# Folding the key projection into the query's, and running the first merge group's projections as three products of halves

## The chip, the core and the metric

The kernel runs on one core of one Trainium2 chip. TensorE (PE) multiplies matrices into PSUM, VectorE (DVE) and ScalarE (ACT) read PSUM and SBUF, GpSimd (POOL) works on SBUF, SyncE (SP) issues most of the transfers. Each engine takes its instructions in the order in which the program lists them, and waits on semaphores for the others. The metric is the device time of the whole kernel in microseconds (us), as a median of runs.

## What is computed

One encoder layer over 1024 tokens of 1024 channels. Only what the change touches is shown; `h` is the normalised input, the chunkwise scan uses `q` and `k` through their inner products and through a state that is a sum of `k v`.

```python
q = jnp.einsum("bshd,hde->bhse", xc, w_q)                    # 4 heads, d = e = 256
k = jnp.einsum("bshd,hde->bhse", xc, w_k) / math.sqrt(d)
v = jnp.einsum("bshd,hde->bhse", xv, w_v)
s = jnp.einsum("bhtd,bhsd->bhts", qc, kc) * w_intra          # in mlstm_scan, chunks of 128
num = w_inter * einsum(qc, C) + einsum(s, vc)                # C_new = decay * C + k w_state v
...
merged = g_m * (y_m @ w_branch_mlstm) + g_l * (y_l @ w_branch_lru)
x = x + merged @ w_out
q = rms_norm(x) @ peer_w_q                                   # 1024 -> 2048, then key scores, top-k
```

## The kernel before

The program is written through a tile framework that orders the instructions of each engine with a model of its own before the run; what stands on each engine is fixed when the kernel is built. All channels lie on the 128 partitions, tokens along the free axis.

**Halves.** Where products must be more exact than one pass of reduced fp32 allows, an operand is split in two: `split` (lines 73 to 79) makes the high half on ACT (or DVE) and the low half, source minus high, on DVE or POOL. `mm3` (lines 81 to 86) then issues three matmuls: high x high (L84), high weight x low (L85), low weight x high (L86). A plain fp32 matmul is one instruction of the program and leaves two records in the trace.

**Weights.** `ws_plan`, `ws_load`, `ws_split` and `ws_get` (lines 89 to 132) stream all weight blocks through a ring of three raw tiles (`wr`) and a ring of high and low tiles (`wh`, `wl`; three deep in the mixers, two deep, `WB2`, from the merge on). A call for block i issues the load of block i + 2 and the split of block i + 1. An entry of the plan that names no engine is handed out raw.

**Mixers.** After the LRU come four mLSTM heads. For each head `ml_x` projects and convolves two 128-channel blocks into `xc`, splits them, and `ml_qkv` makes q, k and v: q and k from one 1024-wide weight tile (`mwq` and `mwk` side by side) with 24 matmuls of 512 columns each, evicted by ACT at line 582, then v with 48 matmuls of 256 columns. `ml_core` runs the chunks; its recurrence leaves PE free at places, and output and merge-gate projections (`ml_o`, `mg`) are put there.

**Merge.** The tokens are then taken in three groups, `GROUPS = [(0, 2), (2, 3), (5, 3)]`, in blocks of 128: group 0 has 256 tokens, the others 384. `merge` runs four projections on a group, with 8, 8, 8 and 16 column blocks of weights (bm, bl, wo, wq), each block eight fp32 matmuls in `mm8` (line 851). Gate tiles, input tiles and keys are loaded beside them by SP. Group 0 runs alone; beside groups 1 and 2 the top-k and one-hot work of dense blocks (`side`) is put on DVE and PE. The dense stage with the gathers, from about 1685 us on, isn't touched.

Of the kernel before, what the change touches and what calls it, by code (L numbers as in the profile page):

```python
# [21 lines left out]
NB = 8  # L22
# [12 lines left out]
class K:  # L35
# [506 lines left out]
    def ml_x(self, h, done=None):  # L542

        nc = self.nc
        st = {}
        st["xm"], st["xc"] = [], []
        for e in range(2):
            blk = 2 * h + e
            x = self.pad_proj(blk, done if e == 0 else None)
            hi, lo = self.u(F32R), self.u(F32R)  # L550
            self.split(x[:, 2:2 + S], hi[:, :S], lo[:, :S])
            st["xm"].append((hi, lo))
            xc = self.u()
            self.conv(xc, x, V_MCW, V_MCB, blk)

            def act(xc=xc):
                nc.scalar.activation(xc[:, :S], xc[:, :S], AF.Silu)
                hi, lo = self.u(F32R), self.u(F32R)
                self.split(xc[:, :S], hi[:, :S], lo[:, :S])
                st["xc"].append((hi, lo))  # L560

            if e == 0:
                act()
            else:
                self.later = act
        return st

    def ml_qkv(self, h, st):
        nc = self.nc
        wh, wl = self.ws_get(("qk", h))  # L570
        for i, nm in enumerate(("q", "k")):
            st[nm] = []
            for e in range(2):
                t = self.u()
                for hf in range(2):
                    c = slice(hf * 512, hf * 512 + 512)
                    p = self.psg()
                    for cb in range(2):
                        o = i * 512 + cb * 256 + e * 128
                        self.mm3(p, (wh[:, o:o + 128], wl[:, o:o + 128]),  # L580
                                 (st["xc"][cb][0][:, c], st["xc"][cb][1][:, c]), cb == 0, cb == 1)
                    nc.scalar.activation(t[:, c], p, AF.Copy, scale=1.0 if i == 0 else 1.0 / 16.0)
                st[nm].append(t)
# [164 lines left out]
    def mixer_plan(self):  # L748
# [29 lines left out]
        for s_ in seq:  # L778
            if s_[0] == "x":
                inw(2 * s_[1])  # L780
                inw(2 * s_[1] + 1)
            elif s_[0] == "o":
                inw(8 + 2 * s_[1])
                inw(9 + 2 * s_[1])
            elif s_[0] == "mg":
                inw(32 + s_[1])
            elif s_[0] == "qkv":
                h = s_[1]
                plan.append((("qk", h), [(self.A["mwq"][h], 512), (self.A["mwk"][h], 512)], 1024, WENG))
# [42 lines left out]
    def merge_items(self, g):  # L832
        A = self.A
        it = []
        for nm, n in (("bm", 8), ("bl", 8), ("wo", 8)) + (("wq", 16),) * len(QSPLIT[g]):
            it += [((nm, g, i), [(A[nm][i], 1024)], 1024, None) for i in range(n)]
        return it

    def load_y(self, src, t0, T):
        r = []  # L840
        for i in range(4):
            t = self.u()
            self.dma = self.nc.sync.dma_start(t[:, :2 * T].rearrange("p (c t) -> p c t", t=T),
                                              src[2 * i:2 * i + 2, :, t0:t0 + T].rearrange("c p t -> p c t"))
            r.append(t)
        return lambda cb: r[cb // 2][:, (cb % 2) * T:(cb % 2) * T + T]

    def mm8(self, p, w, m):

        for cb in range(NB):  # L850
            self.nc.tensor.matmul(p, w[:, cb * 128:cb * 128 + 128], m(cb), start=cb == 0, stop=cb == NB - 1)  # L851

    def merge(self, g, b0, nb):

        nc = self.nc
        T, t0 = nb * 128, b0 * 128
        pair = lambda lst, d: lst[d // 2][:, (d % 2) * T:(d % 2) * T + T]
        y = self.load_y(self.ym_d, t0, T)
        mt = []
        for d in range(NB):  # L860
            if d % 2 == 0:
# [8 lines left out]
        y = self.load_y(self.yl_d, t0, T)  # L870
        for d in range(NB):
            gt = self.u()
            nc.sync.dma_start(gt[:, :T], self.mg_d[8 + d, :, t0:t0 + T])
            w = self.ws_get(("bl", g, d))
            p = self.ps()[:, :T]
            self.mm8(p, w, y)
            nc.vector.tensor_tensor(gt[:, :T], p, gt[:, :T], op=OP.mult)
            nc.vector.tensor_tensor(pair(mt, d), pair(mt, d), gt[:, :T], op=OP.add)
            yield 24 * T * 4.2e-4
        x1, hg = [], []  # L880
        for d in range(NB):
            if d % 2 == 0:
                x1.append(self.u())
                hg.append(self.u())
# [4 lines left out]
            self.mm8(p, w, lambda cb: pair(mt, cb))  # L889
            x = pair(x1, d)  # L890
            nc.vector.tensor_tensor(x, p, xt[:, :T], op=OP.add)
            nc.scalar.activation(pair(hg, d), x, AF.Copy, scale=self.vec(V_G2, d))
            yield 24 * T * 4.2e-4
        rs = self.rs2[:, b0:b0 + nb]
        g2r = []
# [51 lines left out]
        for q0, qn in QSPLIT[g]:  # L947
# [3 lines left out]
            for c in range(16):  # L951
# [7 lines left out]
                self.mm8(p, w, lambda d: pair(hg, d)[:, tq:tq + Tq])  # L959
# [592 lines left out]
def host(**i):  # L1552
# [10 lines left out]
    d["mwq"], d["mwk"], d["mwv"] = hw(a["mlstm_w_q"]), hw(a["mlstm_w_k"]), hw(a["mlstm_w_v"])  # L1563
# [30 lines left out]
```

## Time and profile before

| what | us |
|---|---|
| median of 3 runs (lowest to highest) | 3574.14 (3561.7 to 3575.13) |
| the profiled execution, its own time | 3566.02 |
| its span, first to last instruction | 3563.9 |
| PE busy | 3343.9 (94%) |
| DVE busy | 2929.6 (82%) |
| POOL busy | 1713.4 (48%) |
| ACT busy | 1392.0 (39%) |

The profile is of one execution, and its busy times are averages over stages: the mixers end at about 918 us, group 0 runs from 923 to about 1076 us, groups 1 and 2 to about 1685 us. What a change is worth is read in its own stage. PE's records are pipelined, so the pace of a run of matmuls is read from start to start, or from a row that merges many.

### The profile page before, as it was taken

The page shows a single profiled execution, that of the slowest core. Times are in us where ns is not written, and L with a number is a line of the kernel's source. Part 1 is how long each engine was busy: PE and PEld are TensorE (multiplying, and loading weights), DVE is VectorE, ACT ScalarE, POOL GpSimd, SP SyncE. Part 2 cuts the span into 40 slices and gives each one's busy share as a digit, 9 for nine tenths or more (in the row PEclk, how much of TensorE's full clock was granted, in tenths as well). Part 3 has the DMA queues.
Part 4 walks back from the last instruction along what each step waited for, and adds up shares of the span by engine and source line. Part 5 has one row for each costly group of instructions (what it writes and reads, how often), then busy time and mean ns, then how long its engine had stood idle before and what let it go on. Part 6 is the DMA issues. An engine that isn't in the chain of part 4 may idle for free. (4 is left out here: it accounts for less than half of the span.)

```text
span 3563.9 us, 48538 instructions
## 1 busy us (share of the span) xinstructions
PE 3343.9 (94%) x17633; PEld 2827.0 (79%) x17633; DVE 2929.6 (82%) x5279; ACT 1392.0 (39%) x2565; POOL 1713.4 (48%) x1336
## 2 busy tenths in 40 slices
PE   7999999899899899878899999999999999999998
PEld 5787788778685565556788888998888999999987
DVE  8777574674327866998899999989999999999998
ACT  4565655655120240233333333343333334333333
POOL 7445354444102322342455555655555665666663
PEclk9999999999999999989899999999999999999999
DMA  2122211111466575558888879997887999999996
GB/s 107 60 71 68 72 51 51 63 48 44 154 217 208 159 251 199 174 170 258 312 318 301 283 275 342 360 338 276 314 284 279 341 357 351 344 347 334 352 348 239
DMA packets 319665, 812.56 MB, mean 228 GB/s; under 512 B 25600, under 2 KB 137408, under 8 KB 319424
## 3 DMA queue, kind: packets, MB, share of 16 engines
q0 software_dynamic: 115200, 419.48, 32.4%
q1 hardware_dynamic: 115184, 333.21, 26.7%
q10 hardware_dynamic: 89040, 56.76, 5.3%
q8 instruction: 138, 2.26, 0.3%
q14 instruction: 103, 0.84, 0.1%
HBM read 726.35 MB, written 83.00 MB: 227 GB/s over the span
## 5 line engine op out<-in xcount | busy, mean ns | idle before, releaser
L1334 POOL DMA_INDIRECT k<-in_pv,k x384 | 514.0, 1338 | 378.6 <-DVE k L1365 182.3
L1334 POOL DMA_INDIRECT k<-in_pu,k x384 | 506.6, 1319 | 332.7 <-DVE k L1357 148.0
L84 PE MATMUL ps<-h2h,wh 128*128 128x320 f32 x2048 | 637.2, 312 | 10.2 <-DVE u L1268 9.9
L85 PE MATMUL ps<-h2l,wh 128*128 128x320 f32 x2048 | 635.2, 310 | 0.0
L86 PE MATMUL ps<-h2h,wl 128*128 128x320 f32 x2048 | 628.9, 310 | 5.8 <-DVE wl L71 5.8
L851 PE MATMUL ps<-u,wr 128*128 128x384 f32 (+1 forms) x1920 | 581.1, 460 | 5.5 <-DMA u<-d 3.4
L1357 DVE SCALAR_TENSOR_TENSOR k<-k,rs,k 128x1024 f32<-128x1024 f32 x384 | 493.5, 1289 | 28.4 <-DMA k<-in_pu,k 28.4
L851 PEld LDWEIGHTS ps<-u,wr 128*128 128x128 f32 x1920 | 366.4, 194 | 181.7 <-issue 11.6
L85 PE MATMUL ps<-vl,wdh 128*128 128x512 f32 x1280 | 501.9, 393 | 2.5 <-DVE vl L71 2.5
L84 PE MATMUL ps<-vh,wdh 128*128 128x512 f32 x1280 | 469.0, 395 | 35.1 <-DVE u L1268 17.4
L1365 DVE SCALAR_TENSOR_TENSOR k<-k,k,k 128x1024 f32<-128x1024 f32 x384 | 494.6, 1288 | 0.4
L86 PE MATMUL ps<-vh,wdl 128*128 128x512 f32 x1280 | 494.3, 391 | 0.0
L84 PEld LDWEIGHTS ps<-h2h,wh 128*128 128x128 f32 x2048 | 388.1, 190 | 23.3 <-DVE u L1268 17.0
L86 PEld LDWEIGHTS ps<-h2h,wl 128*128 128x128 f32 x2048 | 385.6, 189 | 8.0 <-DVE wl L71 6.3
L85 PEld LDWEIGHTS ps<-h2l,wh 128*128 128x128 f32 x2048 | 387.8, 189 | 4.5
L1195 ACT ACTIVATE gel<-ps 128x320 f32<-128x320 f32 x256 | 111.1, 435 | 564.2 <-PE ps L86 549.4
L84 PEld LDWEIGHTS ps<-vh,wdh 128*128 128x128 f32 x1280 | 239.3, 189 | 88.2 <-DVE u L1268 22.5
L84 PE MATMUL ps<-h,wh 128*128 128x512 f32 x736 | 292.3, 399 | 14.0 <-ACT u L430 6.7
L86 PE MATMUL ps<-h,wl 128*128 128x512 f32 x736 | 290.8, 396 | 3.5 <-POOL wl L71 3.5
L85 PE MATMUL ps<-h,wh 128*128 128x512 f32 x736 | 291.0, 396 | 2.8 <-DVE h L253 2.8
L1238 ACT ACTIVATE gc<-gt 128x160 f32<-128x160 f32 x512 | 226.3, 510 | 155.9 <-DVE gel L1239 94.4
L86 PEld LDWEIGHTS ps<-vh,wdl 128*128 128x128 f32 x1280 | 241.4, 189 | 50.4
(327 smaller groups left out, 6079.1 us busy)
## 6 DMA issues: line engine op xcount, KB each, us to landing
wr<-in_u SPq DMA_DIRECT2D x128, 512.0 KB
wr<-in_v SPq DMA_DIRECT2D x128, 512.0 KB
d<-stg ACTq DMA_DIRECT2D x40, 1024.0 KB
gt<-d SPq DMA_DIRECT2D x64, 640.0 KB
wr<-in_win SPq DMA_DIRECT2D x49, 512.0 KB
wr<-in_wq SPq DMA_DIRECT2D x48, 512.0 KB
d<-u POOLq DMA_DIRECT2D x32, 512.0 KB
wr<-in_bm SPq DMA_DIRECT2D x24, 512.0 KB
```

Source lines behind the costliest of these rows:

```text
L84: mm(out, wh, mh, start=first, stop=False)
L85: mm(out, wh, ml, start=False, stop=False)
L86: self.lastmm = mm(out, wl, mh, start=False, stop=last)
L851: self.nc.tensor.matmul(p, w[:, cb * 128:cb * 128 + 128], m(cb), start=cb == 0, stop=cb == NB - 1)
L1195: nc.scalar.activation(gel[:, c], p, AF.Gelu)
L1238: nc.scalar.activation(gc[:, i * n:i * n + n], self.gt[j // 8, i][:, :, j % 8], AF.Copy)
L1334: nc.gpsimd.indirect_dma_start(out=t[:, :D], out_offset=None, in_=self.A["pu" if which == "u" else "pv"], in_offset=bass.IndirectOffsetOnA ...
L1357: nc.vector.scalar_tensor_tensor(r[:, :D], r[:, :D], self.rs2[:, b:b + 1], h2[:, :D], op0=OP.mult, op1=OP.mult, accum_out=dots[c][:, k % K ...
L1365: nc.vector.scalar_tensor_tensor(acc[:, :D], r[:, :D], ws[c][:, k % KB:k % KB + 1], acc[:, :D], op0=OP.mult, op1=OP.add)
```

## The change

Two edits. **In the mixers** the weights of q and k are stored transposed, `ml_qkv` multiplies them into one 256 x 256 matrix per head (four fp32 matmuls of 256 columns), ACT and DVE split it from PSUM with the factor 1/16, and q is projected through that matrix; `xc` itself then stands where k stood. The 24 matmuls of k, four of the eight evictions and the split of the 1024-wide weight tile (ACT and POOL) go. **In merge group 0** the weights are split (ACT high, DVE low), and so are the two branch inputs, the merged tiles and the scaled residual, and each fp32 matmul becomes three matmuls of halves. Groups 1 and 2 stay in fp32.

```diff
     def ml_qkv(self, h, st):
-        wh, wl = self.ws_get(("qk", h))
-        for i, nm in enumerate(("q", "k")):
...
-                        o = i * 512 + cb * 256 + e * 128
-                        self.mm3(p, (wh[:, o:o + 128], wl[:, o:o + 128]),
-                                 (st["xc"][cb][0][:, c], st["xc"][cb][1][:, c]), cb == 0, cb == 1)
-                    nc.scalar.activation(t[:, c], p, AF.Copy, scale=1.0 if i == 0 else 1.0 / 16.0)
+        raw = self.ws_get(("qk", h))
+        p = self.psg()
+        for cb in range(2):
+            for eb in range(2):
+                nc.tensor.matmul(p[:, cb * 256:cb * 256 + 256], raw[:, eb * 256 + cb * 128:eb * 256 + cb * 128 + 128],
+                                 raw[:, 512 + eb * 256:512 + eb * 256 + 256], start=eb == 0, stop=eb == 1)
+        t = self.u(F32R)
+        wh, wl = t[:, 0:512], t[:, 512:1024]
+        nc.scalar.activation(wh, p, AF.Copy, scale=1.0 / 16.0)
+        nc.vector.scalar_tensor_tensor(wl, p, 1.0 / 16.0, wh.bitcast(F32), op0=OP.mult, op1=OP.subtract)
...
-                plan.append((("qk", h), [(self.A["mwq"][h], 512), (self.A["mwk"][h], 512)], 1024, WENG))
+                plan.append((("qk", h), [(self.A["mwq"][h], 512), (self.A["mwk"][h], 512)], 1024, None))
...
-            it += [((nm, g, i), [(A[nm][i], 1024)], 1024, None) for i in range(n)]
+            it += [((nm, g, i), [(A[nm][i], 1024)], 1024, "v" if g == 0 else None) for i in range(n)]
...
     def load_y(self, src, t0, T, halves):
+            if halves:
+                hi, lo = self.u(F32R), self.u(F32R)
+                self.split(t[:, :2 * T], hi[:, :2 * T], lo[:, :2 * T])
+                t = (hi, lo)
...
     def mm8(self, p, w, m):
         for cb in range(NB):
-            self.nc.tensor.matmul(p, w[:, cb * 128:cb * 128 + 128], m(cb), start=cb == 0, stop=cb == NB - 1)
+            c = slice(cb * 128, cb * 128 + 128)
+            if isinstance(w, tuple):
+                self.mm3(p, (w[0][:, c], w[1][:, c]), m(cb), cb == 0, cb == NB - 1)
+            else:
+                self.nc.tensor.matmul(p, w[:, c], m(cb), start=cb == 0, stop=cb == NB - 1)
...
+            if halves:
+                if d % 2 == 0:
+                    mhl.append((self.u(F32R), self.u(F32R)))
+                self.split(pair(mt, d), *both(mhl, d))
...
+            if halves:
+                h, l = both(hhl, d)
+                nc.scalar.activation(h, x, AF.Copy, scale=self.vec(V_G2, d))
+                nc.vector.scalar_tensor_tensor(l, x, self.vec(V_G2, d), h.bitcast(F32), op0=OP.mult, op1=OP.subtract)
```

How the instructions stand on the engines, in three places.

PE before, second head: the last filler matmuls (`ps<-h`) and the start of q (`pg<-u` is q or k from the halves of `xc`).

```order
L84 MATMUL ps_4447<-h_444,wh_4228 128x512
L85 MATMUL ps_4447<-h_445,wh_4228 128x512
L84 MATMUL ps_4561<-h_444,wh_4228 128x512
L85 MATMUL ps_4561<-h_445,wh_4228 128x512
L84 MATMUL pg_4022<-u_3799,wh_3877 128x512
L85 MATMUL pg_4022<-u_3800,wh_3877 128x512
L86 MATMUL pg_4022<-u_3799,wl_3878 128x512
```

PE in the changed kernel, second head: the product of the two weight matrices (L576) between filler matmuls.

```order
L84 MATMUL ps_4501<-h_444,wh_4168 128x512
L576 MATMUL pg_3987<-wr_3776 128x256 x4
L85 MATMUL ps_4501<-h_445,wh_4168 128x512
L86 MATMUL ps_4501<-h_444,wl_4169 128x512
L84 MATMUL ps_4501<-h_450,wh_4168 128x512
```

Twenty-three filler matmuls stand between the product and the first q matmul, which reads the folded matrix (`u_3992`):

```order
L85 MATMUL ps_4501<-h_488,wh_4168 128x512
L86 MATMUL ps_4501<-h_487,wl_4169 128x512
L84 MATMUL pg_3996<-u_3769,u_3992 128x512
L85 MATMUL pg_3996<-u_3770,u_3992 128x512
L84 MATMUL pg_4004<-u_3769,u_3992 128x512
```

PE before, group 0, from the third column block of the first projection on: one block after the other (`ps` a block's sum, `wr` its raw weights, `u` the loaded branch input).

```order
L851 MATMUL ps_7947<-u_7905,wr_7916 128x256 x2
L851 MATMUL ps_7947<-u_7907,wr_7916 128x256 x2
L851 MATMUL ps_7947<-u_7909,wr_7916 128x256 x2
L851 MATMUL ps_7947<-u_7911,wr_7916 128x256 x2
L851 MATMUL ps_7961<-u_7905,wr_7930 128x256 x2
```

PE in the changed kernel at the same place: the first two blocks have been interleaved and end together, and the third and fourth (`ps_7891`, `ps_7925`) begin with the products that need only the high weights.

```order
L86 MATMUL ps_7856<-u_7805,wl_7819 128x256
L84 MATMUL ps_7891<-u_7787,wh_7852 128x256
L85 MATMUL ps_7891<-u_7788,wh_7852 128x256
L84 MATMUL ps_7925<-u_7787,wh_7887 128x256
L85 MATMUL ps_7925<-u_7788,wh_7887 128x256
L86 MATMUL ps_7891<-u_7787,wl_7853 128x256
L84 MATMUL ps_7891<-u_7787,wh_7852 128x256
```

DVE before, where group 0 goes from the first to the second projection: only evictions with the gates (L868, L877, L878).

```order
L868 TENSOR_TENSOR u_8000<-ps_8005,u_8001 128x256
L868 TENSOR_TENSOR u_8000<-ps_8019,u_8015 128x256
L877 TENSOR_TENSOR u_8037<-ps_8041,u_8037 128x256
L878 TENSOR_TENSOR u_7913<-u_7913,u_8037 128x256
L877 TENSOR_TENSOR u_8052<-ps_8056,u_8052 128x256
```

DVE in the changed kernel there: low halves of weights (`wl`) and of the second branch input (`u_8092` to `u_8110`) stand between the evictions (L891 is the former L868), in one order.

```order
L71 TENSOR_TENSOR wl_8060<-wr_8023,wh_8059 128x1024
L891 TENSOR_TENSOR u_8020<-ps_8063,u_8055 128x256
L71 TENSOR_TENSOR u_8092<-u_8089,u_8091 128x512
L71 TENSOR_TENSOR wl_8118<-wr_8057,wh_8117 128x1024
L71 TENSOR_TENSOR u_8098<-u_8095,u_8097 128x512
L71 TENSOR_TENSOR u_8104<-u_8101,u_8103 128x512
L71 TENSOR_TENSOR u_8110<-u_8107,u_8109 128x512
L71 TENSOR_TENSOR wl_8157<-wr_8115,wh_8156 128x1024
L71 TENSOR_TENSOR wl_8194<-wr_8154,wh_8193 128x1024
```

The splits of the weights thus share two in-order queues, ACT's and DVE's, with the evictions of the blocks before them.

## Rows read from the trace of the kernel before

**Rows 1.** The page's part 1: busy time of each engine over the span.
```profile
PE 3343.9 (94%) x17633; PEld 2827.0 (79%) x17633; DVE 2929.6 (82%) x5279; ACT 1392.0 (39%) x2565; POOL 1713.4 (48%) x1336
```

**Rows 2.** Windows: stretch, length, busy PE PEld DVE ACT POOL, PE clock, DMA, GB/s.
```profile
405.00:435.00 30.00, 30.00 (x157) 25.58 (x156) 9.67 (x15) 18.66 (x42) 11.04 (x12) 1.00 0.39 106
435.00:485.00 50.00, 50.00 (x296) 44.25 (x295) 32.08 (x78) 29.09 (x73) 27.00 (x33) 1.00 0.15 48
...
923.00:1076.00 153.00, 149.91 (x723) 132.03 (x724) 27.62 (x109) 21.88 (x48) 6.88 (x10) 0.99 0.66 222
...
1320.00:1360.00 40.00, 40.00 (x157) 25.82 (x156) 10.64 (x66) 9.40 (x16) 0.00 (x0) 1.00 0.70 237
1360.00:1600.00 240.00, 205.03 (x949) 129.94 (x948) 233.45 (x748) 47.02 (x88) 85.97 (x65) 0.92 0.56 179
```

**Rows 3.** Timeline of PE, second head: start, duration; two of k's matmuls, first and last of 18 of v's.
```profile
554.41 0.39 PE L84 MATMUL pg<-u,wh 128*128 128x512 f32 x1
554.64 0.39 PE L85 MATMUL pg<-u,wh 128*128 128x512 f32 x1
...
556.73 0.28 PE L84 MATMUL pg<-wh,u 128*128 128x256 f32 x1
...
558.72 0.28 PE L86 MATMUL pg<-wh,u 128*128 128x256 f32 x1
```

**Rows 4.** Timeline of PE, group 0: its start, and a long merged run.
```profile
923.25 9.19 PE L851 MATMUL ps<-u,wr 128*128 128x256 f32 x32 [1.31 <-DMA u<-d]
...
959.80 25.42 PE L851 MATMUL ps<-u,wr 128*128 128x256 f32 x117
```

**Rows 5.** Groups of 923 to 1076 us: count, busy, mean ns of one, idle before and its releasers.
```profile
L851 PE MATMUL ps<-u,wr 128*128 128x256 f32 x640 | 142.2, 383 | 4.2 <-DMA u<-d 3.4 <-DMA wr<-in_bm 0.8
...
L960 ACT ACTIVATE u<-ps 128x256 f32<-128x256 f32 x16 | 6.1, 382 | 30.7 <-PE ps L851 30.7
...
L891 DVE TENSOR_TENSOR u<-ps,u 128x256 f32<-128x256 f32 x8 | 3.4, 425 | 24.2 <-DMA u<-in_xT 12.1 <-PE ps L851 8.7 <-PE ps L906 3.5
L868 DVE TENSOR_TENSOR u<-ps,u 128x256 f32<-128x256 f32 x8 | 3.3, 424 | 29.5 <-DMA u<-d 16.9 <-PE ps L851 12.6
```

**Rows 6.** Waits of SP's queue in group 0: total us, times, longest.
```profile
SPq L101 <- PE ps L851: 88.9, 34, 5.6
```

**Rows 7.** Groups of the dense stage: the weight split, low half on DVE.
```profile
L71 DVE TENSOR_TENSOR wl<-wr,wh 128x1024 fp32r<-128x1024 f32 x126 | 153.9, 1222 | 27.1 <-ACT wh L78 26.3 <-issue 0.6
```

**Rows 8.** Groups of the dense stage on ACT: the high half.
```profile
L78 ACT ACTIVATE wh<-wr 128x1024 fp32r<-128x1024 f32 x126 | 133.0, 1055 | 121.1 <-DMA wr<-in_u 121.1
```

**Rows 9.** Groups from 0 to 1300 us: ACT and DVE reading PSUM, 512 wide.
```profile
L582 ACT ACTIVATE u<-pg 128x512 f32<-128x512 f32 x32 | 18.6, 593 | 15.2 <-PE pg L86 14.9
...
L731 DVE SCALAR_TENSOR_TENSOR u<-pg,c,u 128x512 f32<-128x512 f32 x16 | 11.1, 744 | 0.6 <-PE pg L729 0.5
```

**Rows 10.** Timeline of PE before the first head, after a wait.
```profile
356.24 0.80 PE L84 MATMUL ps<-u,wh 128*128 128x512 f32 x1 [4.54 <-ACT u L78]
...
362.31 0.63 PE L84 MATMUL ps<-u,wh 128*128 128x512 f32 x1
362.74 0.63 PE L85 MATMUL ps<-u,wh 128*128 128x512 f32 x1
```

**Rows 11.** Windows of the same place (columns as in Rows 2).
```profile
356.00:364.00 8.00, 6.50 (x13) 4.33 (x14) 3.53 (x2) 6.56 (x10) 2.05 (x4) 0.50 0.36 133
```

**Rows 12.** Timeline of SP: the second head's q weights are issued.
```profile
436.90 0.33 SPq L101 DMA_DIRECT2D wr<-in_mwq  x1
```

**Rows 13.** Timeline of ACT, first head: the last mask exponentials.
```profile
418.64 2.45 ACT L621 ACTIVATE u<-u,c 128x128 f32<-128x128 f32 x8
```

**Rows 14.** Timeline of DVE, first head: the first use of these masks.
```profile
436.80 1.29 DVE L641 TENSOR_TENSOR u<-pg,u 128x512 f32<-128x512 f32 x2 [2.84 <-PE pg L638]
```

**Rows 15.** Waits of DVE from 1057 to 1690 us: for the scores of a group.
```profile
DVE s L1000 <- DMA x<-d: 63.0, 4, 33.0
```

**Rows 16.** Waits of PE from 1057 to 1690 us: for one-hot tiles.
```profile
PE pg L1116 <- DVE g L1098: 26.7, 10, 4.4
```

More of the change, by code (lines that the diff above doesn't have):

```diff
@@ L545, in ml_x @@
         st = {}
-        st["xm"], st["xc"] = [], []
+        st["xm"], st["xc"], st["k"] = [], [], []
         for e in range(2):
@@ L560, in act @@
                 st["xc"].append((hi, lo))
+                st["k"].append(xc)
             if e == 0:
@@ L569, in ml_qkv @@
         nc = self.nc
-        wh, wl = self.ws_get(("qk", h))
-        for i, nm in enumerate(("q", "k")):
[L572 to L578, printed above, removed]
-                        o = i * 512 + cb * 256 + e * 128
-                        self.mm3(p, (wh[:, o:o + 128], wl[:, o:o + 128]),
-                                 (st["xc"][cb][0][:, c], st["xc"][cb][1][:, c]), cb == 0, cb == 1)
-                    nc.scalar.activation(t[:, c], p, AF.Copy, scale=1.0 if i == 0 else 1.0 / 16.0)
-                st[nm].append(t)
+        raw = self.ws_get(("qk", h))
[8 more added lines that the diff above has]
+        nc.vector.scalar_tensor_tensor(wl, p, 1.0 / 16.0, wh.bitcast(F32), op0=OP.mult, op1=OP.subtract)
+        st["q"] = []
+        for e in range(2):
+            t = self.u()
+            for hf in range(2):
+                c = slice(hf * 512, hf * 512 + 512)
+                p = self.psg()
+                for cb in range(2):
+                    o = cb * 256 + e * 128
+                    self.mm3(p, (wh[:, o:o + 128], wl[:, o:o + 128]),
+                             (st["xc"][cb][0][:, c], st["xc"][cb][1][:, c]), cb == 0, cb == 1)
+                nc.scalar.activation(t[:, c], p, AF.Copy)
+            st["q"].append(t)
         wh, wl = self.ws_get(("v", h))
@@ L835, in merge_items, with load_y @@
         for nm, n in (("bm", 8), ("bl", 8), ("wo", 8)) + (("wq", 16),) * len(QSPLIT[g]):
-            it += [((nm, g, i), [(A[nm][i], 1024)], 1024, None) for i in range(n)]
+            it += [((nm, g, i), [(A[nm][i], 1024)], 1024, "v" if g == 0 else None) for i in range(n)]
         return it
-    def load_y(self, src, t0, T):
+    def load_y(self, src, t0, T, halves):
         r = []
@@ L844, in load_y @@
                                               src[2 * i:2 * i + 2, :, t0:t0 + T].rearrange("c p t -> p c t"))
+            if halves:
+                hi, lo = self.u(F32R), self.u(F32R)
+                self.split(t[:, :2 * T], hi[:, :2 * T], lo[:, :2 * T])
+                t = (hi, lo)
             r.append(t)
-        return lambda cb: r[cb // 2][:, (cb % 2) * T:(cb % 2) * T + T]
+        part = lambda t, cb: t[:, (cb % 2) * T:(cb % 2) * T + T]
+        if halves:
+            return lambda cb: tuple(part(t, cb) for t in r[cb // 2])
+        return lambda cb: part(r[cb // 2], cb)
     def mm8(self, p, w, m):
         for cb in range(NB):
-            self.nc.tensor.matmul(p, w[:, cb * 128:cb * 128 + 128], m(cb), start=cb == 0, stop=cb == NB - 1)
+            c = slice(cb * 128, cb * 128 + 128)
[3 more added lines that the diff above has]
+                self.nc.tensor.matmul(p, w[:, c], m(cb), start=cb == 0, stop=cb == NB - 1)
     def merge(self, g, b0, nb):
         nc = self.nc
-        T, t0 = nb * 128, b0 * 128
+        T, t0, halves = nb * 128, b0 * 128, g == 0
         pair = lambda lst, d: lst[d // 2][:, (d % 2) * T:(d % 2) * T + T]
-        y = self.load_y(self.ym_d, t0, T)
+        both = lambda lst, d: tuple(t[:, (d % 2) * T:(d % 2) * T + T] for t in lst[d // 2])
+        mhl, hhl = [], []
+        y = self.load_y(self.ym_d, t0, T, halves)
         mt = []
@@ L869, in merge @@
             yield 24 * T * 4.2e-4
-        y = self.load_y(self.yl_d, t0, T)
+        y = self.load_y(self.yl_d, t0, T, halves)
         for d in range(NB):
@@ L883, in merge @@
                 x1.append(self.u())
-                hg.append(self.u())
+                if halves:
+                    hhl.append((self.u(F32R), self.u(F32R)))
+                else:
+                    hg.append(self.u())
             xt = self.u()
@@ L888, in merge @@
             p = self.ps()[:, :T]
-            self.mm8(p, w, lambda cb: pair(mt, cb))
+            self.mm8(p, w, lambda cb: both(mhl, cb) if halves else pair(mt, cb))
             x = pair(x1, d)
             nc.vector.tensor_tensor(x, p, xt[:, :T], op=OP.add)
-            nc.scalar.activation(pair(hg, d), x, AF.Copy, scale=self.vec(V_G2, d))
+            if halves:
+                h, l = both(hhl, d)
+                nc.scalar.activation(h, x, AF.Copy, scale=self.vec(V_G2, d))
+                nc.vector.scalar_tensor_tensor(l, x, self.vec(V_G2, d), h.bitcast(F32), op0=OP.mult, op1=OP.subtract)
+            else:
+                nc.scalar.activation(pair(hg, d), x, AF.Copy, scale=self.vec(V_G2, d))
             yield 24 * T * 4.2e-4
@@ L958, in merge @@
                 p = self.ps()[:, :Tq]
-                self.mm8(p, w, lambda d: pair(hg, d)[:, tq:tq + Tq])
+                self.mm8(p, w, lambda d: tuple(t[:, tq:tq + Tq] for t in both(hhl, d)) if halves else pair(hg, d)[:, tq:tq + Tq])
                 nc.scalar.activation(qp(qt, c), p, AF.Copy)
@@ L1562, in host @@
     hw = lambda m: f(m[0].reshape(H, 2, 128, 256).transpose(0, 2, 1, 3).reshape(H, 128, 512))
-    d["mwq"], d["mwk"], d["mwv"] = hw(a["mlstm_w_q"]), hw(a["mlstm_w_k"]), hw(a["mlstm_w_v"])
+    ht = lambda m: hw(m.reshape(1, H, 256, 256).transpose(0, 1, 3, 2))
+    d["mwq"], d["mwk"], d["mwv"] = ht(a["mlstm_w_q"]), ht(a["mlstm_w_k"]), hw(a["mlstm_w_v"])
     lw = lambda m: f(m[0].transpose(1, 2, 0, 3).reshape(8, 128, 256))
```

## The prediction

> **What bounds the kernel now.** I began with the busy times of the whole span: PE works 94% of it and DVE 82% [rows 1]. That average says nothing of the two places that change, so I read the windows of each. In the first head's q, k and v PE is busy without a gap from 405 to 485 us at full clock, while DVE and ACT have room [rows 2]. Merge group 0 is the same: 149.9 of 153 us on PE, but only 27.6 on DVE, 21.9 on ACT and 6.9 on POOL [rows 2]. There, matmul time is the time of the stage. Transfers are not: SP's queue of weight loads waited 88.9 us for PE to give a buffer back [rows 6], and PE's idle time before the fp32 matmuls was 4.2 us in all, nearly all of it at the start [rows 5]. So both edits take work from the engine that bounds its stage, and the question is what the added splits put in its place.
>
> **The mixers, term by term.** One 512-column matmul takes the pace from start to start, 554.64 - 554.41 = 0.23 us [rows 3]. Each head loses the 24 of k: 24 x 0.23 = 5.5 us. It gains four fp32 matmuls of 256 columns, two records each. A long run of such records took 25.42 us for 117, so 0.217 each [rows 4], and eight cost 1.7 us. Net 3.8 us a head, 15 us in four heads.
>
> What else the edit does lies off the path. The product must be read by ACT (one reading of 512 columns, 0.59 us) and then by DVE (0.74 us) [rows 9], 1.3 us before q can start. On PE 23 filler matmuls stand between the product and q in the second head, 23 x 0.23 = 5.3 us, so 4 us are to spare; without the filler each head would pay the 1.3 us and the product's share of the gain would be gone. The product reads raw weights, which are earlier than split ones: the second head's were issued at 436.90 us, 105 us before its q [rows 12]. Four evictions of 0.59 us go from ACT, and POOL loses a 1024-wide subtraction per head; neither was waited for. What comes sooner after q and k must not be met by a late mask: in the first head the last exponentials began at 418.64 and took 2.45 us [rows 13], their first use was at 436.80 after a wait for PE [rows 14]. That leaves 15 us where 5.5 are needed.
>
> [...] Downward, the cores behind have idle PE time, and where a recurrence on other engines sets the end, early PE work buys nothing; I let it fall to 8 us.
>
> **Group 0, term by term.** A column block was 16 records, 16 x 0.217 = 3.48 us [rows 4]. Now it is 24 products of halves of 256 columns. The same form stands in v: 18 of them started from 556.73 to 558.72, 17 steps of 0.117 us [rows 3]. 24 x 0.117 = 2.81 us. Forty blocks save 40 x 0.67 = 27 us on PE. [...]
>
> [...]
>
> Now the price of the splits. A weight block costs ACT 1.06 us [rows 8] and DVE 1.22 us [rows 7], measured in the dense stage, where the same form runs; forty make 42 and 49 us, on engines that were busy 22 and 28 of 153 [rows 2]. In bulk there is room. In order there is less, for three reasons.
>
> First, the ring of halves has two slots. Block k + 1 can be split only when block k - 1 has left PE, and then PE has just block k, 2.81 us, to hide ACT's 1.06 and DVE's 1.22. In the last projection ACT also evicts the earlier block, 0.38 us [rows 5]. That is 2.66 us and the handovers between three engines, as near to 2.81 as can be. I take 0.25 us a block for sixteen blocks, 4 us; the bounds are 0, and 0.8 a block.
>
> Second, where a projection starts, two blocks are interleaved and end together. Both slots then come free at once, and PE waits for a whole split, 1.06 + 1.22 = 2.28 us, less the four products that need only high weights, 0.47: 1.8 us. The order shows this at the start of bm, and the same at bl, wo and wq: 4 x 1.8 = 7 us.
>
> Third, the inputs. The first branch input arrives at 923 us and PE starts on it at once [rows 4]; now a 512-wide high half (0.59) and a low half (two 512-wide ones took 1.29 [rows 14], so 0.65) come first: 1.2 us. At the second projection three of the four inputs are split behind the weight block that must wait for its slot: 1.5 us. The merged tiles and the residual are split 256 wide, 0.4 us each on either engine, in time that DVE has.
>
> Together 14 us, so group 0 gives back 27 - 14 = 13 us. Bounds: 27 if all is hidden; -8 if the waits repeat at most blocks. The transfers get 512 KB a block in 2.81 instead of 3.48 us. At 222 GB/s and a DMA share of 0.66 [rows 2], a fifth more is 0.8: I cost it at nothing.
>
> **What passes on.** Behind group 0 DVE waits for scores, 63 us in four waits [rows 15], 33 of them around 1320 to 1360 us where PE is full and DVE nearly empty [rows 2]; so group 1 on PE carries a gain forward, and from 1360 to 1600 us DVE, full at 233 of 240 us [rows 2], starts sooner by as much. DVE's splits at the end of group 0 push the first top-k back by some six splits, 7 us, and PE does wait for one-hot tiles, 26.7 us [rows 16]; but the later empty stretch of DVE takes that up.
>
> The sum against the profiled execution's own 3566 us (span 3563.9): 3566 - 15 - 13 = **3538 us**. The median of the three runs is 8 us above that execution, so 3546 would be the same result seen from there.
>
> **Rivals.** *The splits pace group 0.* Evictions stand on DVE before the low halves, in one order, and they wait for gate and input tiles: DVE idled 16.9 us for gates and 12.1 for input tiles [rows 5], harmless then, since only PSUM was held. If such waits now hold up splits, the 13 us are gone, and the mixers alone give 3551 us. For it: these waits. Against it: the loads that were late stood behind weight loads held by PE [rows 6], and those now go when a split is done. [...]
>
> *The mixers' gain is lost in the cores*, and group 0 gives 13: 3553 us. Against it: PE was full through q, k and v.
>
> [...]
>
> *Slower.* One mechanism: ACT, DVE and PE take turns in group 0, because the two slots and the in-order queues never let a split run beside the block before it. A block then takes 2.81 + 2.28 = 5.09 us, 40 x 1.61 = 64 us more than before; less 15 it ends at 3615. It decides from 3.48 + 15/40 = 3.86 us a block. Against it: away from the starts the order leaves a whole block of products beside each split.
>
> *The fold does nothing to PE*, since q's own halves are late: it isn't likely, as before q and k ran back to back with no idle time.
>
> **How the numbers follow.** My forecast, both gains with the splits half hidden, 3526 to 3548 us: 58%. All hidden: 6%. Splits pace group 0: 20%. Mixers' gain lost: 8%. Slower by the turns, or part of the way there: 8%. The range has the forecast, the all-hidden case's nearer half and the two cases near 3552, with the 8 us by which the shown median lies higher: 3522 to 3564; the forecast's own range is 3526 to 3548. About 0.5%, 18 us, is what can be told from no change: faster 62% (the first two cases, less 2 for the forecast's edge), the same 30% (the two middle rivals and that edge), slower 8%.
>
> **What would show it.** In the changed profile: 512-column `pg<-u` products 24 a head instead of 48, eight 256-column records of L576, and no wait of the first q product for DVE beyond 1 us; group 0's stretch near 138 us instead of 153, DVE's low halves at 1.2 us, PE idle of 1 to 2 us at four starts for `wl`; groups 1 and 2 as long as before. A group 0 above 150 us makes the first rival true, above 165 us the slower one; mixers shorter by under 8 us make the second. The forecast fails too if the clock in group 0 falls at the new waits, for at 0.43 us a matmul [rows 10] a few us of gain go at each.

## The result and the profile after

The changed kernel takes 3534.15 us (median of 4 runs, 3527.58 to 3535.14) against 3574.64 (4 runs): ratio 0.989, 95% interval 0.9863 to 0.9917. The profiled execution has a span of 3532.8 us, 31.1 less than before. The total is 4 us from the forecast, 3538 us, which was summed from the profiled execution of before; seen from the median of before, the same forecast was 3546. Its parts are not the forecast's, and most of this section and the next is about that.

Page part 1 of the changed kernel, for [rows 1]: PE is busy 26 us less, DVE 67 and ACT 41 us more.

```profile
PE 3317.8 (94%) x17889; PEld 2818.7 (80%) x17889; DVE 2996.5 (85%) x5347; ACT 1432.7 (41%) x2605; POOL 1718.1 (49%) x1332
```

Windows of the changed kernel (columns as in [rows 2]): the first head's q and v, and group 0.

```profile
430.00:480.00 50.00, 50.00 (x291) 44.02 (x291) 32.27 (x80) 28.51 (x73) 25.94 (x33) 1.00 0.17 48
903.80:1053.80 150.00, 136.39 (x1047) 131.14 (x1046) 86.49 (x172) 65.04 (x100) 9.89 (x10) 0.95 0.70 230
```

The mixers are as full as before and shorter. Group 0 is not full any more: PE idles 13.6 of 150 us, where it idled 3.1 of 153, DVE has three times its work, and the granted clock fell from 0.99 to 0.95.

Three places divide the span: the fourth head's first score product (q times k, L638 before, L648 now), the first 384-column matmul (where group 1 begins), and the first second-layer product of the dense stage. Times in us:

| | fourth head's scores | group 1 begins | dense stage | end |
|---|---|---|---|---|
| before | 834.8 | 1076.3 | 1742.9 | 3563.9 |
| changed | 816.1 | 1053.8 | 1714.5 | 3532.8 |
| difference | -18.7 | -22.5 | -28.4 | -31.1 |

So the mixers gave 18.7 us, the stretch with group 0 some 4 (3.1 of it in group 0 itself, from its first block 153.0 us before and 149.9 now), and 8.6 came behind group 0, where nothing was changed. Between the medians the drop is 40.5 us, more than the 31.1 of the two profiles: the profiled execution of before lies 8 us below its median.

Waits of PE in the changed kernel, 903 to 1053 us: total, times, longest. For [rows 5], where it waited 4.2 us in all: 2.1 at the start of group 0 and 2.05 at the start of the second projection.

```profile
PE ps L84 <- ACT wh L78: 5.9, 9, 0.9
PE ps L1003 <- DMA u<-in_keys: 2.4, 2, 2.0
PE ps L86 <- DVE wl L71: 1.6, 3, 0.7
PE ps L84 <- ACT u L78: 1.3, 2, 1.0
PE ps L84 <- DVE u L741: 1.1, 1, 1.1
PE ps L85 <- DVE u L71: 1.0, 2, 0.8
```

Groups of the same stretch: on either engine the weight split's idle time is the ring of two slots, seen from its two sides.

```profile
L71 DVE TENSOR_TENSOR wl<-wr,wh 128x1024 fp32r<-128x1024 f32 x38 | 47.4, 1252 | 29.0 <-ACT wh L78 28.9
L78 ACT ACTIVATE wh<-wr 128x1024 fp32r<-128x1024 f32 x38 | 40.0, 1058 | 46.6 <-PE ps L85 36.2 <-DMA wr<-in_wq 4.7 <-issue 4.6
```

ACT idles 36.2 us until PE gives a slot back, DVE 28.9 until ACT is done: PE, ACT and DVE take turns there.

Two kinds of wait are not the ring's. The three waits of PE for low halves of weights (`wl`, 1.6 us) each come behind a late tile: on DVE the split stands behind evictions that had waited 2.2, 1.5 and 3.1 us for a gate or an input tile. The first of them:

```profile
920.78 0.42 DVE L891 TENSOR_TENSOR u<-ps,u 128x256 f32<-128x256 f32 x1 [2.23 <-DMA u<-d]
921.75 0.43 DVE L891 TENSOR_TENSOR u<-ps,u 128x256 f32<-128x256 f32 x1 [0.55 <-DMA u<-d]
922.10 1.21 DVE L71 TENSOR_TENSOR wl<-wr,wh 128x1024 fp32r<-128x1024 f32 x1
```

And at 1032 to 1038 us loads are late. SP stood 5.6 us before a load of scores (`x<-d`), until their store had landed; the keys and the next wq weights stood behind it and were issued after 1029 us, and PE waited for the keys, ACT for the weights. Waits of SP from 1015 to 1040 us, and timelines of SP, PE and ACT:

```profile
SPq L1049 <- DMA d<-u: 5.6, 1, 5.6
1022.90 0.34 SPq L101 DMA_DIRECT2D wr<-in_wq  x1
1028.90 0.33 SPq L1049 DMA_DIRECT2D x<-d  x1
1029.32 0.52 SPq L991 DMA_DIRECT2D u<-in_keys  x1
...
1030.41 0.43 SPq L101 DMA_DIRECT2D wr<-in_wq  x1
1034.62 1.71 PE L1003 MATMUL ps<-u,u 128*128 128x128 f32 x12 [1.96 <-DMA u<-in_keys]
1036.55 1.06 ACT L78 ACTIVATE wh<-wr 128x1024 fp32r<-128x1024 f32 x1 [4.68 <-DMA wr<-in_wq]
```

Timeline of PE, start of the third projection (wo): two waits for high halves, then the pace.

```profile
966.57 0.28 PE L86 MATMUL ps<-u,wl 128*128 128x256 f32 x1
966.69 0.28 PE L85 MATMUL ps<-u,wh 128*128 128x256 f32 x1
...
969.44 0.38 PE L84 MATMUL ps<-u,wh 128*128 128x256 f32 x1 [0.84 <-ACT wh L78]
969.66 0.28 PE L85 MATMUL ps<-u,wh 128*128 128x256 f32 x1
970.39 0.39 PE L84 MATMUL ps<-u,wh 128*128 128x256 f32 x1 [0.45 <-ACT wh L78]
...
972.07 0.41 PE L84 MATMUL ps<-u,wh 128*128 128x256 f32 x1
972.29 0.41 PE L85 MATMUL ps<-u,wh 128*128 128x256 f32 x1
...
975.06 0.28 PE L84 MATMUL ps<-u,wh 128*128 128x256 f32 x1
975.18 0.28 PE L85 MATMUL ps<-u,wh 128*128 128x256 f32 x1
```

Start to start is 0.12 us before the waits, 0.22 at 972, and 0.12 again from 975. Behind the waits the granted clock was 0.51, from 971 to 974.5 us. Windows of the changed kernel show a fall at two other places too, at the start (0.53 from 904 us) and at 1036 us (0.52), beside an undisturbed stretch (1.00 from 924 us):

```profile
904.00:910.00 6.00, 4.91 (x23) 4.32 (x22) 3.21 (x5) 0.00 (x0) 1.10 (x2) 0.53 0.43 175
924.00:934.00 10.00, 10.00 (x86) 10.00 (x86) 6.30 (x8) 3.18 (x3) 0.00 (x0) 1.00 0.80 256
970.00:975.00 5.00, 4.61 (x25) 4.60 (x26) 2.17 (x3) 0.73 (x2) 0.00 (x0) 0.66 0.62 176
1036.00:1043.00 7.00, 6.11 (x30) 5.81 (x30) 7.00 (x33) 2.60 (x4) 0.00 (x0) 0.52 0.74 267
```

### The profile page after: what moved, and what is told of

The parts are those of the page before. It is cut to its first block, busy times and chain, and to the rows that moved or that the text cites. A ratio compares the mean times of both kernels' runs of the same rounds, so it can differ in the third digit from the quotient of the medians.

```text
span 3532.8 us, 49184 instructions
## 1 busy us (share of the span) xinstructions
PE 3317.8 (94%) x17889; PEld 2818.7 (80%) x17889; DVE 2996.5 (85%) x5347; ACT 1432.7 (41%) x2605; POOL 1718.1 (49%) x1332
## 4 chain that ended last, share of the span: by engine, by line
PE 56%; DVE 26%; DMA 7%; issue 6%; ACT 3%; POOL 1%; ACTq 0%; SPq 0%; DVEq 0%; POOLq 0%
PE ps L84 15%; PE ps L85 15%; PE ps L86 15%; PE ps L872 5%; DVE k L1392 3%; DVE k L1400 2%; DMA k<-in_pu,k 2%; DMA wr<-in_u 2%; DVE u L1303 1%; DVE wl L71 1%; DVE s L1092 1%; DVE g L1137 1%; PE pg L84 1%; PE pg L85 1%; PE pg L86 1%
## 5 line engine op out<-in xcount | busy, mean ns | idle before, releaser
L872 PE MATMUL ps<-u,wr 128*128 128x384 f32 x1280 | 440.2, 500 | 3.4 <-DVE u L901 3.4
L872 PEld LDWEIGHTS ps<-u,wr 128*128 128x128 f32 x1280 | 244.7, 196 | 162.6 <-issue 13.1
L78 ACT ACTIVATE wh<-wr 128x1024 fp32r<-128x1024 f32 (+1 forms) x202 | 211.5, 1048 | 228.9 <-DMA wr<-in_u 151.0
## 6 DMA issues: line engine op xcount, KB each, us to landing
gt<-d SPq DMA_DIRECT2D x64, 640.0 KB, 10.5
```

The costliest lines, as they stand in the source:

```text
L78: self.nc.scalar.activation(hi, src, AF.Copy)
L872: self.nc.tensor.matmul(p, w[:, c], m(cb), start=cb == 0, stop=cb == NB - 1)
```

## The experiments

Each kernel is timed against the kernel before (ratio with its 95% interval); in the profile of each, one execution, I read where group 1 begins and how long it is from there to the end. That stretch holds the same work in all kernels but the one with halves in all groups.

| kernel | us | group 1 begins | from there to the end |
|---|---|---|---|
| before | 3570 to 3575 | 1076.3 | 2487.6 |
| changed | 3534.2 | 1053.8 | 2479.0 |
| fold alone | 3536.7 | 1059.6 | 2476.0 |
| halves alone | 3538.1 | 1071.6 | 2460.7 |
| changed, three slots | 3531.2 | 1047.0 | 2484.2 |
| the same, placed elsewhere | 3531.5 | 1046.7 | 2483.8 |
| before, pad of 4 | 3559.1 | 1073.5 | 2484.6 |
| before, pad of 20 | 3562.8 | 1082.6 | 2475.8 |
| before, pad of 40 | 3563.2 | 1092.0 | 2469.5 |
| changed, pad of 30 | 3532.9 | 1055.1 | 2476.3 |
| three slots, pad of 46 | 3514.1 | 1046.2 | 2465.4 |
| one weight block | 3508.5 | 1042.5 | 2466.0 |
| halves in all groups | 3587.4 | 1055.5 | 2534.3 |

**The fold alone.**

```diff
-            it += [((nm, g, i), [(A[nm][i], 1024)], 1024, "v" if g == 0 else None) for i in range(n)]
+            it += [((nm, g, i), [(A[nm][i], 1024)], 1024, None) for i in range(n)]
...
-        T, t0, halves = nb * 128, b0 * 128, g == 0
+        T, t0, halves = nb * 128, b0 * 128, False
```

> The fold alone: group 0 is back to fp32 matmuls of raw weights. My theory: the mixers gave 17.8 us in the changed kernel (last mLSTM output at 900.2 instead of 918.0 us) and that comes from the fold alone, so the mixers end near 900, group 0 takes 153 us again, and the span is 18 to 21 us shorter than before (about 3544, ratio 0.995). A rival: the fold's gain is lost behind the mixers (top-k and the dense stage have their own pace) and only part of it reaches the end: less than 10 us. Another: the 31 us between the two spans is mostly the fold's, with what it sets free behind it: 25 us or more.

Ratio 0.9901 (0.9887 to 0.9915). Group 1 begins 16.7 us sooner, but the total is 35 us shorter: my theory has the front right, and the rival of a gain behind it has the total.

**The halves alone.** `ml_qkv`, its weights and its plan entry are again those of before the change.

> Group 0 in halves alone: the mixers are as before the change, with the key projection. My theory: group 0, from its first block to the first matmul of group 1, falls from 153 to about 150 us, as in the changed kernel, so the total is 3 to 8 us shorter than before (ratio 0.998 to 0.999). The prediction's step would have it 13 us shorter (0.996). The rival, that the splits' waits cost more than the products save, gives 0 or slower.

Ratio 0.9912 (0.9899 to 0.9926). Group 1 begins 4.7 us sooner, as my theory had it, with group 0 at 146.6 us from its first block; the total is 34 us shorter, which nothing here had expected. At the place where group 1 begins the two parts add up (16.7 + 4.7 against 22.5). At the end they don't: 35 and 34 alone, 36 to 40 together. What lies behind group 0 answers to something else than time saved.

**A third slot of halves.** Every third weight block of group 0 takes a pair of tiles of its own.

```diff
+            elif key[0] in ("bm", "bl", "wo", "wq") and self.ws_ns % 3 == 2:
+                hi = self.wx.tile([128, 1024], F32R, name=self.name("wh"), tag="hx", bufs=1)
+                lo = self.wx.tile([128, 1024], F32R, name=self.name("wl"), tag="lx", bufs=1)
...
+        kk.wx = al(name="wx", bufs=1, side="right")
```

> The changed kernel with a third slot for high and low halves in the merge (every third block takes a tile pair of its own). Theory A, two slots pace the starts: blocks no longer begin in pairs with the products of high weights, the waits of PE for high weight halves (9 waits, 5.9 us, and 1.3 for inputs) fall below 3 us, the clock's falls behind them go, and group 0 takes 138 to 143 us instead of 150; the total is 7 to 12 us below the changed kernel, ratio 0.986 to 0.987 against before. Theory B, the in-order queues of ACT and DVE and the late inputs set these waits: group 0 stays within 3 us of 150 and the ratio at 0.989.

Ratio 0.9886 (0.9871 to 0.9901). Theory A holds for group 0: from its first block to group 1 136.6 us, PE waits 1.1 us in two waits for high weight halves instead of 5.9 in nine, and the clock doesn't fall again after the start (granted 1.00 from 914 us to the end of group 0). But the first block began only at 910.4 us, after 7.7 us of waiting for its input, and of the 6.8 us by which group 1 is sooner than in the changed kernel the total shows 3: theory A's total, 7 to 12 lower, did not come.

**The third slot placed elsewhere.** The same program, with `wx` on the other side of memory (without `side="right"`).

> Three slots once more, with the same order of instructions as the run with three slots, but the third pair of tiles lies behind the other buffers of the merge, so that the tiles for the inputs lie where they lay in the changed kernel. There PE waited 7.7 us for the split of the first branch input, whose load was issued at 906.6 us instead of before 900. My theory: the load waited for memory of the mixers that was still read, and goes early again here; the start wait falls under 3 us, group 1 begins 5 to 7 us sooner (near 1041 us) and the total is 3 to 7 us below the kernel with three slots (3524 to 3528, ratio 0.9865 to 0.988). The rival, that the order of SP's queue held the load, leaves all as it was.

Ratio 0.9885 (0.987 to 0.9901). The first block begins at 904.1 us, so the load had waited for memory, not for SP's order. Yet group 1 begins at 1046.7, where it began: the total is the rival's, though its mechanism is not. The trace shows where the 6 us went: 3.1 to a fall of the clock from 970.6 to 977.4 us (granted 0.57 in the window from 970 to 978), 1.1 to a wait for the mixers' last eviction (L744), some 2 to longer waits for halves of inputs. The kernel with three slots has no such fall, although PE waited as long there (1.4 and 0.6 us in both); why the clock fell in the one alone is not settled. Waits of PE in this kernel, 903 to 1046 us:

```profile
PE ps L84 <- ACT u L78: 2.8, 2, 1.4
PE ps L1006 <- DMA u<-in_keys: 1.5, 2, 1.2
PE ps L85 <- DVE u L71: 1.4, 2, 1.2
PE ps L86 <- DVE wl L71: 1.3, 2, 0.8
...
PE ps L84 <- ACT wh L78: 0.6, 1, 0.6
```

Windows of this kernel at the fall, and of the kernel with three slots from 914 us to the end of group 0:

```profile
970.00:978.00 8.00, 7.23 (x35) 6.73 (x35) 5.07 (x7) 3.98 (x5) 0.00 (x0) 0.57 0.50 154
914.00:1047.00 133.00, 125.25 (x1031) 122.51 (x1030) 81.93 (x167) 64.83 (x100) 8.11 (x8) 1.00 0.73 241
```

**One weight block for all.** `ws_split` hands out the halves of the first block forty times, so the weights of the other blocks are left out.

```diff
+            if key[0] in ("bm", "bl", "wo", "wq") and self.one is not None:
+                self.ws_hl[self.ws_ns] = self.one
```

> The changed kernel with the halves of one weight block used for all forty blocks of group 0: the splits of the other blocks on ACT and DVE are left out, and so is the use of their weights (their loads are issued but never waited for). What is left of group 0 is its products, the splits of its inputs and the evictions. My theory: the splits of weights and the clock's falls behind them are 12 to 18 us of group 0's 150, so group 1's first matmul comes 132 to 138 us after the first block; products alone, 1045 records of 0.1185 us, are 124. The rival, that inputs, gates and keys hold group 0 back: 143 us or more.

Ratio 0.9827 (0.9813 to 0.984). Group 0 takes 139.5 us from its first block: 10.5 less than the changed kernel, a little less than I had set, so inputs have a part in it. PE still waits 3.1, 3.0 and 1.1 us for DVE's evictions. The two long ones had themselves waited for late tiles, of a gate and of the residual's input:

```profile
959.29 0.79 DVE L907 TENSOR_TENSOR u<-ps,u 128x256 f32<-128x256 f32 x2 [4.80 <-DMA u<-d]
977.58 0.75 DVE L928 TENSOR_TENSOR u<-ps,u 128x256 f32<-128x256 f32 x2 [5.26 <-DMA u<-in_xT]
```

At each the clock fell (granted 0.57 from 960 to 964 us and 0.54 from 977 to 984.5). So without the splits of weights group 0 is paced, at two places, by the late tiles that the prediction's first rival names. Net of that, all the splits of weights together cost about what the third slot gave back (7 us), and 3 more.

**Halves in all groups.** `halves = True` and `"v"` for every group.

> Halves in all three groups. In groups 1 and 2 a block of fp32 takes 16 records of 384 columns at 0.325 us, 5.2 us; 24 products of halves at an estimated 0.17 us (three halves of 0.117 for 256 columns) would be 4.1, so 80 blocks would save about 88 us on PE. But DVE is busy 512 of the 605 us there and would get 80 low halves of 1.22 us, 98 us, and the splits of inputs. My theory: DVE becomes the bound, the stretch takes at least 630 us and the total is 20 to 60 us longer than the changed kernel (ratio 0.995 to 1.006). The rival, that PE bounds these groups too and DVE's work fits into its idle time, gives 30 to 80 us less than the changed kernel.

Ratio 1.0044 (1.0027 to 1.006), 53 us above the changed kernel: my theory, near the upper end of its range. PE's longest wait in groups 1 and 2 of this kernel, and DVE's split there:

```profile
PE ps L86 <- DVE wl L71: 31.0, 22, 5.3
```

```profile
L71 DVE TENSOR_TENSOR wl<-wr,wh 128x1024 fp32r<-128x1024 f32 x80 | 114.1, 1429 | 16.1 <-ACT wh L78 16.1
```

The products took 0.175 us, 24 of them 4.2 against 5.2 us, as expected; here, with DVE busy 573 of 625 us, they buy nothing.

**Useless matmuls in the kernel before.** Pads of 4, 20 and 40 save nothing and change what the framework's model sees.

```diff
         y = self.load_y(self.ym_d, t0, T)
+        if g == 0:
+            pad = self.ps()
+            for i in range(4):
+                nc.tensor.matmul(pad[:, :256], self.ident, y(0), start=True, stop=True)
```

> The kernel before, with four useless fp32 matmuls of 256 columns at the start of group 0 (eight records of 0.217 us, 1.7 us of PE work more) and nothing else. The framework then orders the instructions of groups 1 and 2 and of the dense stage in another way than before: about the order that it also gives to the fold alone and to the halves alone. Theory C, the order behind group 0 is worth as much as the edits: the time from group 1's first matmul to the end falls by 10 to 25 us, as in those two kernels, though nothing was saved, and the total is 8 to 23 us below before (ratio 0.994 to 0.998). Rival D, the gain behind group 0 comes from the earlier start alone: the total is 1 to 3 us above before (ratio 1.0003 to 1.001).

> The kernel before with forty such useless matmuls, 80 records of 0.217 us, 17.4 us of PE work. Here the order behind group 0 stays near that of before (as many instructions of DVE and ACT lie behind group 1's first matmul). Theory C: about 12 to 20 us longer than before (ratio 1.003 to 1.006), since the delay is passed on and the order is not much better or worse. Rival D: the delay would shrink behind group 0 as the gains grew there; 17 us here would cost 17 to 35 (1.005 to 1.010). Rival E, there is slack behind group 0 that hides changes in front: under 8 us (below 1.002).

> The kernel before with twenty useless fp32 matmuls in group 0, sixteen (6.9 us of PE work) more than the pad of four, with nearly the same order behind group 1's first matmul (113 of 3215 places of DVE differ, none of SP). Theory C: group 1 begins 6 to 8 us later than with the pad of four (1073.5) and the delay reaches the end: 3562 to 3569, ratio 0.9975 to 0.9995. Rival E, slack behind group 0 takes the delay up: 3556 to 3561, ratio 0.996 to 0.997.

The pad of 4 makes the kernel 12 us faster, 0.9963 (0.9949 to 0.9976), which is theory C's total; but in the two profiles only 3.0 us of it lie behind group 1, not 10 or more. The pad of 40, with 17.4 us of useless work in front, is 8 us faster than before, 0.998 (0.9971 to 0.9989), and here 18.1 us lie behind. No theory had that number: theory C's own forecast and rival D, both with a loss, fall, rival E's bound holds, and for theory C my premise was wrong, since the order behind group 1's beginning had changed with that pad too (2169 of DVE's 4165 records there, by the two traces). The pad of 20, with nearly the order of the pad of 4, is 3.7 us above it, 0.998 (0.9971 to 0.9989): inside theory C's range. But in the profiles group 1 begins 9.1 us later and the end comes 0.3 us later, so this pair doesn't decide against rival E.

**A pad in the changed kernel.** The same with thirty products of high halves.

> The changed kernel with thirty useless products of high halves, 256 columns each, in group 0: 30 times 0.117, 3.5 us of PE work more. The order behind group 0 becomes the one that the fold alone and the halves alone have. Theory C: that order is worth 5 to 15 us behind group 1's first matmul against the changed kernel's own, so the total falls by 2 to 12 us, to 3522 to 3532 (ratio 0.9855 to 0.9885). Rival D: 3 to 5 us longer, 3537 to 3539 (ratio 0.990).

Ratio 0.9886 (0.987 to 0.9901), 3532.9 us: 1 us outside theory C's range and 4 below rival D's. Against the changed kernel that is too near to tell anything. Against the fold alone it tells something: by the two traces the records behind group 1's beginning stand in nearly the same order (33 of PE's 12805 places and 3 of DVE's 4165 differ, none on ACT, POOL and SP), group 1 begins 4.5 us sooner, the median is 3.8 us lower, and the stretch to the end takes 2476.3 us against 2476.0. The two kernels with three slots, one order, agree as well (2484.2 and 2483.8).

**Three slots and a pad of 46.** Here the order of instructions from group 1 on is that of the halves alone.

> The changed kernel with three slots and forty-six useless products of high halves in group 0 (46 times 0.117, 5.4 us of PE work). With this pad the order of instructions from group 1's first matmul on is, but for 22 places, that of the halves alone, where the stretch from there to the end took 2460.7 us, the shortest of all. Theory C, the order sets the length behind: group 1 begins near 1052 us (1046.8 with three slots, and 5.4) and the end comes 2455 to 2467 us later, at 3507 to 3519, ratio 0.982 to 0.986: faster than every kernel so far in spite of the pad. Rival E, something behind group 0 holds the end near 3531 to 3536 whatever the front gains (as six kernels have it, with group 1 beginning from 1046.8 to 1071.6 us): ratio 0.988 to 0.990, and the stretch behind is 2475 to 2485 us.

Ratio 0.9847 (0.9834 to 0.9861), 3514.06 us: the fastest of those that leave nothing out. Its total and its stretch behind (2465.4 us) are theory C's, though group 1 begins at 1046.2 and not near 1052; rival E falls. Windows of this kernel from group 1's beginning, in two parts, and then of the kernel with three slots and no pad, placed in the same way:

```profile
1046.20:1701.20 655.00, 580.66 (x3015) 389.51 (x3013) 545.93 (x1666) 165.38 (x304) 208.46 (x152) 0.94 0.66 211
1701.20:3511.60 1810.40, 1767.73 (x9792) 1599.76 (x9792) 1719.21 (x2500) 683.13 (x1218) 1048.74 (x790) 0.99 0.89 322
```

```profile
1046.70:1708.30 661.60, 580.09 (x3016) 390.70 (x3015) 554.37 (x1666) 166.23 (x304) 209.78 (x152) 0.94 0.66 208
1708.30:3530.50 1822.20, 1772.79 (x9792) 1602.65 (x9792) 1718.28 (x2500) 684.49 (x1218) 1047.07 (x790) 0.99 0.89 320
```

Group 1 begins within 0.5 us, the counts on every engine agree, and the first is 6.6 us shorter in groups 1 and 2 and 11.8 us in the dense stage. What differs is the order: by the two traces, in 2245 of DVE's 4165 places and in 22 of SP's 527. And against the halves alone, where the order is the same but for 22 places, group 1 begins 25.4 us sooner and the median is 24.0 us lower (20.7 between the two profiles): with the order held, a gain in front reaches the end, nearly whole.

## Why the prediction was right, and where it was not

**The total**, 3538 against 3534, was right through terms that missed in both directions: 15 + 13 + 0 predicted, 18.7 + 4 + 8.6 in the profile. That is luck twice: what group 0 lacked came from behind it, where nothing had been forecast, and the sum started from an execution 8 us below its kernel's median; between the medians the drop is 40.5 us, not 28.

**The mixers: right, above the 15 us and far from the 8 to which they were let fall.** The four heads gave 6.0, 3.7, 3.9 and 5.1 us (by each one's first score product); 3.8 had been worked out, and the fourth's surplus was not followed up. The range's lower end, 3522 us, leans on the all-hidden case; no run shows how much the mixers give when all is hidden, and what the runs showed is 18.7 us in the changed kernel and 16.7 with the fold alone, where group 1 begins. In the first head the product stands at a place where PE had waited 4.54 us [rows 10]. Timeline of PE in the changed kernel there:

```profile
351.06 1.02 PE L576 MATMUL pg<-wr 128*128 128x256 f32 x4
355.77 0.50 PE L84 MATMUL ps<-u,wh 128*128 128x512 f32 x1 [3.69 <-ACT u L78]
356.11 0.59 PE L576 MATMUL pg<-wr 128*128 128x256 f32 x2
357.68 0.79 PE L84 MATMUL ps<-u,wh 128*128 128x512 f32 x1 [0.98 <-ACT u L430]
```

The product lies in and around that idle time and costs next to nothing, where 1.7 us had been set; the clock fell there all the same (granted 0.57 from 356 to 364 us, 0.50 before). In the other heads its eight records ran in one piece, 539.53 to 541.0 us in the second, 0.22 each, as costed.

**Group 0: the step that failed, by late transfers and the clock.** The saving was nearly right: 24 products at 0.1185 us are 2.84 a block, against 2.81 set, so 25 us for forty blocks instead of 27: 18% less than fp32's 3.48 a block. The stalls were set at 14. PE waited 9.8 us in sixteen waits for splits and 1.1 in one for the mixers' last eviction (L741), and each of these 17 costs some 0.25 us beyond its idle time, another 4: the whole 0.28 us of the last product before a wait go by, where the next usually starts after 0.12, and the first step behind it is 0.22 us. So the 14 were there, even a little more, in other shares. At the starts PE waited for high halves rather than for low ones, and the third slot took most of these waits away. The last projection's sixteen blocks, set at 4 us, had one wait of 0.9 beyond its start.

What was costed at nothing is the rest. The transfers were put at nothing because their rate had room. The rate did have room on average (DMA share 0.70 in group 0), but the order of SP's queue issued loads late: PE waited 2.4 us for keys, 2.0 of them behind the load of scores, and at 1037 us for a high half whose weights came late behind the same load. And the clock: the prediction named a fall at the new waits as what would make it fail, and gave it no price. Besides the one at the start, which [rows 4] also had (32 records in 9.19 us, 0.29 each, granted 0.78 from 923 to 933 us), there were two falls, some 10 us at half pace (granted 0.51 from 971 to 974.5 us and 0.50 from 1036 to 1042.6), which cost 4 us by the starts of the products: 1.5 at 971 us, behind waits for splits, and 2.6 at 1036 us, behind the late keys. With the 2 us of the smaller saving that makes some 8 of the 9 us by which 13 came out as 4. The halves alone bear out the clock's part: there PE waits 14 us after the first block, against 13 here, but the clock stays up once the start is over (1.00 against 0.96 in the windows below), and group 0 takes 146.6 us instead of 149.9. A window of that kernel, and the same stretch of the changed one:

```profile
929.60:1071.60 142.00, 127.80 (x1026) 122.70 (x1025) 83.39 (x167) 65.26 (x99) 8.77 (x8) 1.00 0.73 237
909.70:1053.80 144.10, 131.58 (x1028) 126.92 (x1028) 83.28 (x167) 65.04 (x100) 8.79 (x8) 0.96 0.71 232
```

Group 0 at 149.9 us stands on the border of the first rival (150). Its mechanism, splits held up by evictions that wait for tiles, is in the trace, with the three waits for `wl`, 1.6 us. The prediction had read PE's 4.2 us of idle time before as nearly all at the start; 2.05 of them were a wait for a tile at the second projection, so late tiles were not quite harmless there either.

**What passes on: right with the order held, wrong as used.** The prediction passed the front's gains on one for one and left groups 1, 2 and the dense stage as they were. The framework ordered them anew in every kernel, and for the same work they took 2460.7 to 2487.6 us, with the kernel before at the long end. That the order alone moves the end by such amounts is shown by the pair with three slots, and in the medians by the pad of 4, where nothing was saved; and pairs with one order took the same stretch to within 0.3, 0.4 and 4.7 us (the pads of 4 and 20, with nearly one order, to 8.8). That the changed kernel's own 8.6 us are order too is argued from there, and they are no more than single executions differ by (those of the kernel before lay between 3561.7 and 3579.2). For the halves alone it is 26.9 of the 31.6 us between the profiles, for the fold alone 11.6 of 28.3. Which of the moved instructions costs most isn't settled; in the pair, PE's busy time differs by 4.5 us behind group 1 and DVE's by 7.5, so most of the 18.4 us is waiting.

**The other rivals.** The slower one stayed away: 150 us for forty blocks are 3.75 us a block with all waits, just below the 3.86 from which it decides. In groups 1 and 2, with halves in all groups and DVE busy 573 of 625 us, splits did hold PE (31 us for `wl`); whether by turns or because DVE was full is not separated.

## What to carry to other kernels

When a program's order is made by a scheduler, compare the order behind the place that you changed before you credit the change with its total: a control that saves nothing (a few useless instructions) tells how much of the time is order. Price a new wait with what surrounds it: here each cost its idle time, a quarter of a microsecond beside it, and at two places 1.5 and 2.6 us at a granted clock of 0.51 and 0.50. When a stage gets shorter, follow the loads that feed it through the queue that issues them. And where the products interleave two blocks, try a ring of split operands with a third slot: here it took the waits for high halves from 5.9 us to about 1, and group 1 began 7 us sooner.

## What the runs showed that was not expected

Four useless matmuls, 1.7 us of work, made the kernel 12 us faster (3559.1 against 3570.9); 5.4 us of them, with three slots, made it 17 us faster (3514.1 against 3531.5). The same 128 x 1024 subtraction on DVE took 1252 ns in group 0 and, with halves in all groups, 1429 in groups 1 and 2, where POOL was busy 199 of 625 us instead of 10 of 150; whether that is the cause was not tried.
